# A two-layer hybrid encoder on one core: bias sums taken early, transposes of value blocks deferred, gate stores issued by GpSimd

## The chip, the core and the metric

The kernel runs on one core of a Trainium2 chip. A core has a matrix engine (TensorE; the profile has PE for its products and PEld for its weight loads), three engines for element-wise work (VectorE, in the profile DVE; ScalarE, ACT; GpSimd, POOL), SyncE (SP), which here only issues transfers, and 16 DMA engines. Each engine carries out its own instructions in their order, and waits on semaphores for the others. The metric is the time of one execution on the device in microseconds (us); of several runs the median is given.

## The reference

The program is two layers of a bidirectional encoder over 512 tokens of width 1024. Cut to what matters here:

```python
h = x
for l in range(DEPTH):                                   # 2 layers
    h = h + 0.5 * rmsnorm(swiglu(rmsnorm(h, ..), ..), ..)
    u = rmsnorm(h, mix_pre_g[l])
    qa, ka, va, qb, kb, vb, qc, kc, vc, gl = split(u @ w_in[l])   # one projection
    oa = neighbourhood_attention(qa, ka, va, na_rpb[l])  # 8 heads of 64, bias and mask added to scores
    ob = sliding_window_attention(rope(qb), rope(kb), vb, sw_sink[l])
    oc = differential_attention(rope(qc), rope(kc), vc, ...)
    yb = einsum(stack([oa, ob, oc]), w_branch[l])
    merged = sum(sigmoid(gl + b_gate[l]) * yb, axis=2)   # three gates of width 1024
    h = h + rmsnorm(merged @ w_out[l], mix_post_g[l])
    h = h + 0.5 * rmsnorm(swiglu(rmsnorm(h, ..), ..), ..)
```

In the neighbourhood attention the bias of a head is looked up by the distance of query and key on a grid of 8 by 64 tokens, and keys outside a window of 16 columns are masked with -1e30. `sigmoid(z)` is computed as (1 + tanh(z/2))/2, so a gate is one tanh on ScalarE.

## The kernel before

All values are float32. A product of two float32 matrices is made of three products: each operand is split into a high part and what is left of it, a low part, and high x high, low x high and high x low are added up in a PSUM bank (L326, L327 and L328 in one helper, L680 in another). ScalarE makes the high parts, VectorE the low ones.

A layer goes through four phases, each with a pool of memory of its own: the first feed-forward part, the projection (`project`), the mixer (`mixer`) and the second feed-forward part. In the profiled execution the projection of the first layer lies at about 370 to 510 us and its mixer at 508 to 860; those of the second layer at 1545 to 1690 and 1690 to 2040.

**The projection.** The 30 column blocks of 128 for queries, keys and values are made here. Eight of them (`COVER`) are plain products, the other 22 go in 11 groups of two blocks (`GROUPS`), by a scheme with seven products in place of eight (class `Seven`, products p1 to p7, L680). Its sums need many more steps on VectorE: sums of weights (L621, L640, L644) and low parts (L630, L654, L658, L667), and sums of products (L733, L738). PSUM has eight banks: two "mm", two "mx", three "at" and one "o". During the groups two of the "at" banks hold sums of the groups (`seed_banks`), so one is left for everything else.

A finished block is copied out of PSUM by ScalarE in halves or whole (`evict`, L1398) and handed to `ready`. Blocks of queries and keys are split and stored in DRAM for later (`stacked`, `store`, whose stores GpSimd issues at L1405). Value blocks (VA, VB, VC) go through `turned`: four transposes on PE into a bank "at" (L1432), and then a copy to a high part by ScalarE (L1438) and a subtraction on VectorE (L1439) for each of two halves, and stores. Blocks of the second branch that need a rotation put four steps into a list `slowly`; after each group `work(3)` runs three steps of that list, and what is left is run when the last group is done. `tables_of_a`, called in group 6's turn, loads a tile `pre` of tag "n" (two buffers, outside the phases' pools): the masks (L1549, L1550) and the bias tables of heads 0 and 1 (L1552).

**The mixer.** The table `ORDER` sets the order in which its units are written: `qa1` loads the operands of two heads of the neighbourhood attention (branch a), `aa1` is that attention, `kb`, `qb`, `ab` and `qc`, `ac`, `fc` belong to branches b and c, `ga3` is block 3 of gate a, `ya3` block 3 of the merge of branch a. A unit for two heads of branch a (`qkv_a`) asks for the bias tables of its heads (`ask`, tile `braw`, L1726; for heads 0 and 1 they are in `pre`), then loads its stacks: operands `st` whose upper half is the high part and whose lower half is the low part, four transfers of 128 KB a head, at L1776 and L1777 (`restacked`), and the value parts `x` (L1753). `biases` adds bias and mask with four steps on VectorE (L1737), into two tiles of the mixer's pool. `softmax_pv` then makes the scores (L1672), adds the bias and takes the maximum (L1675), takes the exponential (L1684 on ScalarE) and divides by the sum (L1692, or L1694 on VectorE); its second half, run after the next head's scores, transposes the probabilities (L1703), splits them (L352 and L353) and multiplies by the values (L1706, L1707). For the other branches a rotation loads a block and a copy with halves swapped (`sh`, L1761) and combines them (L1762 to L1764).

A gate block is a product of 24 matrix steps (L326 to L328) and one tanh (L1909). Gate a's blocks stay on chip, in two tiles of tag "n". The blocks of gates b and c are stored in DRAM, 256 KB each, by SP at L1912, 16 a layer, and loaded back when they are merged (`combine`; the sums of branch b on GpSimd at L1926).

**What sets the order.** The kernel is written as one sequence; a scheduler then decides the order of each engine's instructions, and adds the waits. A transfer issued by SP, ACT or GpSimd stands in that engine's order, and if it must wait, for its data, for its buffer, or for an earlier transfer that uses the same completion semaphore, everything behind it on that engine waits too. Weight loads (`wr`, L211) are issued by SP in the projection and by ACT in the mixer.

## Time and profile before

| | us |
|---|---|
| median of 3 runs (2383.48 to 2388.46) | 2384.1 |
| the profiled execution | 2380.2 |
| its span | 2378.4 |
| PE busy in the span | 2346.9 |
| DVE busy | 1883.2 |
| ACT busy | 1448.5 |
| POOL busy | 178.8 |

The span goes from the first to the last instruction of the profiled execution; some 1.8 us lie around it. Rows of a timeline read: start, duration, engine, line, operation, output and inputs, and in square brackets how long the engine was idle before and what released it. In a table of waits a row reads: who waited, for what, total us, times, longest. "SPq" and "ACTq" are transfers that the engine issues. The engine order below is of the built program and has no times in it.

### The profile page before, as it was taken

What the parts mean: (1) busy time and instruction counts of PE and PEld (TensorE: products, weight loads), DVE (VectorE), ACT (ScalarE), POOL (GpSimd) and SP (SyncE); (2) the same over time, 40 slices, a digit from 0 to 9 for tenths busy, and PEclk for the clock granted to TensorE, in tenths of its full rate; (3) what the DMA queues carried; (4) which work ended last, traced back from release to release, by engine and by line L of the source; (5) the groups of instructions that cost most, each with busy time, mean ns of one, the idle gap of its engine ahead of it and who ended that gap; (6) DMA issues with size and microseconds to landing.
All of it is one profiled execution on the core that took longest, in us unless ns stands there. A gap on an engine that the chain in (4) does not pass through costs nothing. (4 is left out here: it accounts for less than half of the span.)

```text
span 2378.4 us, 39981 instructions
## 1 busy us (share of the span) xinstructions
PE 2346.9 (99%) x15062; PEld 2105.4 (89%) x15062; DVE 1883.2 (79%) x3056; ACT 1448.5 (61%) x2711; POOL 178.8 (8%) x242
## 2 busy tenths in 40 slices
PE   9999999999999999999999999999999999999998
PEld 8999889987888789998899998899878878899987
DVE  7887987967977577888878878889589766788796
ACT  6565566668766365655655554666687664556563
POOL 0111001110000101110001110011000010011100
PEclk9999999999999999999999999999999999999999
DMA  5566446667565534664525565376766664346642
GB/s 170 161 169 192 153 142 197 207 205 214 164 186 177 158 100 141 170 159 166 174 87 169 160 178 195 107 218 207 210 188 175 171 201 131 106 144 170 192 144 87
DMA packets 143264, 395.13 MB, mean 166 GB/s; under 512 B 19296, under 2 KB 26080, under 8 KB 142560
## 3 DMA queue, kind: packets, MB, share of 16 engines
q1 hardware_dynamic: 114672, 279.25, 37.8%
q0 software_dynamic: 12992, 57.68, 9.4%
q10 hardware_dynamic: 15408, 55.66, 7.7%
q8 instruction: 118, 1.93, 0.3%
q14 instruction: 74, 0.61, 0.1%
HBM read 326.98 MB, written 80.74 MB: 171 GB/s over the span
## 5 line engine op out<-in xcount | busy, mean ns | idle before, releaser
L680 PE MATMUL mm<-X,h 128*128 128x256 f32 x1472 | 261.6, 277 | 0.2
L224 ACT ACTIVATE w<-wr 128x512 fp32r<-128x512 f32 x272 | 167.7, 627 | 119.9 <-PE mm L328 67.9
L225 DVE TENSOR_TENSOR w<-wr,w 128x512 fp32r<-128x512 f32 x272 | 190.9, 710 | 59.7 <-ACT w L224 58.8
L326 PE MATMUL mm<-X,w 128*128 128x512 f32 (+1 forms) x602 | 228.5, 380 | 2.0 <-ACT X L553 1.8
L327 PE MATMUL mm<-X,w 128*128 128x512 f32 (+1 forms) x602 | 227.8, 378 | 0.8 <-DVE X L554 0.7
L328 PE MATMUL mm<-X,w 128*128 128x512 f32 (+1 forms) x602 | 226.4, 377 | 0.0
L680 PEld LDWEIGHTS mm<-X,h 128*128 128x128 f32 x1472 | 223.6, 188 | 1.2 <-DVE v L738 0.5
L680 PE MATMUL mm<-ht,l 128*128 128x256 f32 x736 | 205.9, 280 | 0.0
L680 PE MATMUL mm<-ht,h 128*128 128x256 f32 x736 | 205.5, 279 | 0.0
L680 PE MATMUL mm<-lt,h 128*128 128x256 f32 x736 | 204.8, 278 | 0.0
L680 PE MATMUL mx<-ht,h 128*128 128x256 f32 x736 | 203.7, 277 | 0.0
L680 PE MATMUL mx<-lt,h 128*128 128x256 f32 x736 | 203.6, 277 | 0.0
L680 PE MATMUL mm<-X,l 128*128 128x256 f32 x736 | 203.6, 277 | 0.0
L680 PE MATMUL mx<-ht,l 128*128 128x256 f32 x736 | 203.4, 276 | 0.0
L630 DVE TENSOR_TENSOR l<-wr,h 128x1024 fp32r<-128x1024 f32 x92 | 112.5, 1223 | 62.7 <-PE mm L680 62.6
L662 ACT ACTIVATE h<-wr 128x1024 fp32r<-128x1024 f32 x92 | 97.7, 1062 | 73.6 <-PE mx L680 52.6
L680 PE MATMUL at<-X,w 128*128 128x256 f32 x1104 | 141.1, 277 | 0.0
L680 PEld LDWEIGHTS mm<-ht,l 128*128 128x128 f32 x736 | 138.7, 188 | 0.1
L680 PEld LDWEIGHTS mm<-lt,h 128*128 128x128 f32 x736 | 138.7, 188 | 0.0
L680 PEld LDWEIGHTS mm<-ht,h 128*128 128x128 f32 x736 | 138.6, 188 | 0.0
L680 PEld LDWEIGHTS mx<-lt,h 128*128 128x128 f32 x736 | 138.3, 188 | 0.0
L680 PEld LDWEIGHTS mx<-ht,h 128*128 128x128 f32 x736 | 138.1, 188 | 0.2
(449 smaller groups left out, 6748.2 us busy)
## 6 DMA issues: line engine op xcount, KB each, us to landing
wr<-in_wts_dram SPq DMA_DIRECT2D x269, 512.0 KB
wr<-in_wts_dram ACTq DMA_DIRECT2D x106, 512.0 KB
sum<-in_wts_dram POOLq DMA_DIRECT2D x64, 512.0 KB, 4.9
st<-part SPq DMA_DIRECT2D x120, 128.0 KB
ap<-in_wts_dram SPq DMA_DIRECT2D x20, 512.0 KB
a<-kept SPq DMA_DIRECT2D x32, 256.0 KB
ap<-sum SPq DMA_DIRECT2D x16, 512.0 KB
x<-part SPq DMA_DIRECT2D x32, 256.0 KB
```

The source lines that it names most:

```text
L224: A.activation(hi, raw, AF.Copy)
L225: V.tensor_tensor(out=lo, in0=raw, in1=f(hi), op=ALU.subtract)
L326: PE.matmul(acc, w[0], x[0], start=start, stop=False)
L327: PE.matmul(acc, w[0], x[1], start=False, stop=False)
L328: PE.matmul(acc, w[1], x[0], start=False, stop=stop)
L630: V.tensor_tensor(out=w["l1"], in0=self.raws[g][0], in1=f(w["h1"]), op=ALU.subtract)
L662: A.activation(self.W[g]["h24"], self.raws[g][1], AF.Copy)
L680: PE.matmul(acc, ws[i], xs[j], start=start and k == m == 0, stop=stop and k == n - 1 and m == 2, skip_group_check=True,)
```

## The change

The diff has five parts: (1) in `ORDER`, the first two gate blocks are gb0 and gb1, and ga0, ga1 and others follow later; (2) the bias sums of heads 0 and 1 go into a new tile `edges`, the second tile of tag "n", in place of tiles of the mixer's pool; (3) `qkv_a` asks for bias tables after the stacks and values; (4) the stores of gates b and c are issued by GpSimd; (5) `turned` for value blocks is put in the list `slowly`.

```diff
--- before.py
+++ after.py
@@ -70,8 +70,8 @@
 
 
 ORDER = """
-qa0 qa1 aa0 ga0 ga1 qa2 aa1 ga2 qa3 aa2 ga3 gb0 kb qb0 aa3 gb1 qb1 ab0
-gb2 gb3 qb2 ab1 gb4 gb5 gb6 qb3 ab2 gb7 ga4 qc0 ab3 ga5 ga6 qc1 ac0
+qa0 qa1 aa0 gb0 gb1 qa2 aa1 ga0 qa3 aa2 ga1 ga2 kb qb0 aa3 ga3 gb2 qb1
+ab0 gb3 qb2 ab1 gb4 gb5 gb6 qb3 ab2 gb7 ga4 qc0 ab3 ga5 ga6 qc1 ac0
 ga7 ya0 gc0 ya1 qc2 fc0 ac1 gc1 ya2 gc2 ya3 gc3 fc1 qc3 ac2 ya4 ya5
 ya6 ya7 yb0 gc4 fc2 ac3 yb1 gc5 yb2 gc6 fc3 yb3 gc7 yb4 yb5 yb6 yb7
 yc0 yc1 yc2 yc3 yc4 yc5 yc6 yc7
@@ -1467,9 +1467,9 @@
             elif QB <= c < VB:
                 turned_by(c, x)
             elif c < QB or c == VB:
-                turned(c, x, 2)
+                slowly.append(lambda: turned(c, x, 2))
             elif c >= VC:
-                turned(c, x, 1)
+                slowly.append(lambda: turned(c, x, 1))
             else:
                 made[c] = store("raw", x)
 
@@ -1551,6 +1551,7 @@
             for hd in range(2):
                 nc.sync.dma_start(t[:, 2 + hd, :], raw_of(l, hd))
             made["tables"] = t
+            made["edges"] = sb.tile([P, 4, T], F32, tag="n", name=nm("edges"), bufs=BUFS["n"])
 
         def gate_tile(c):
             if (c - GL) % 4 == 0:
@@ -1727,8 +1728,12 @@
 
         def biases(hd):
             raw = raws.pop(hd)
-            edge = big("g", name="bedge")
-            mid = big("g", shape=(P, 2 * P), name="bmid")
+            if hd < 2:
+                edge = made["edges"][:, hd, :]
+                mid = made["edges"][:, 2, 2 * P * hd : 2 * P * (hd + 1)]
+            else:
+                edge = big("g", name="bedge")
+                mid = big("g", shape=(P, 2 * P), name="bmid")
 
             def put(dst, mask, n0, n1):
 
@@ -1799,9 +1804,10 @@
 
 
         def qkv_a(p):
+            got = restacked(QA + p, False), restacked(KA + p, True), values(VA + p)
             for s in range(2):
                 ask(2 * p + s)
-            return restacked(QA + p, False), restacked(KA + p, True), values(VA + p)
+            return got
 
         oa = [sb.tile([P, 4, T], F32R, tag="X", name=nm("oa"), bufs=BUFS["X"]) for _ in range(2)]
 
@@ -1909,7 +1915,7 @@
                 A.activation(t, pg, AF.Tanh, scale=0.5, bias=col("b_gate", l, n * KD + m))
                 if n:
                     d = dr.tile([P, T], F32, tag="gate", name=nm("gate"), bufs=4 * KD)
-                    nc.sync.dma_start(d, t)
+                    G.dma_start(d, t)
                     t = d
                 gate[n, m] = t
```

How this moves instructions is seen at three places. Lines behind the edited ones have numbers higher by one to six after the change (L1737 becomes L1742, L1726 becomes L1727, L1753 L1758, L1761 L1766, L1776 and L1777 L1781 and L1782, L1912 L1918). The numbers in names are those of buffers and tell the same tile of another; names of the two programs can't be compared by number.

**PE, transposes of the last deferred groups of the first layer's projection.** Before, a block (x803) is transposed in two pairs, as its halves come:

```order
L680 MATMUL mm791_5230<-X539_3649,h24785_5213 128x256
L680 MATMUL mm791_5230<-X538_3648,l24793_5245 128x256
L1432 MATMUL at819_5417<-cons_66,x803_5331 128x128 x2
L680 MATMUL mm811_5363<-ht2608_4128,h24806_5351 128x256
L680 MATMUL mm811_5363<-lt2609_4129,h24806_5351 128x256
L1432 MATMUL at819_5417<-cons_66,x803_5331 128x128 x2
L680 MATMUL mm811_5363<-ht2608_4128,l24813_5378 128x256
```

After, the block (x804) and the block of values with it are transposed four at a time, one after the other, behind other products:

```order
L680 MATMUL mm826_5486<-ht1595_4069,h13817_5398 128x256
L680 MATMUL mm826_5486<-lt1596_4070,h13817_5398 128x256
L680 MATMUL mm826_5486<-ht1595_4069,l13821_5433 128x256
L1432 MATMUL at845_5615<-cons_66,x804_5332 128x128 x4
L1432 MATMUL at850_5628<-cons_66,v799_5269 128x128 x4
L680 MATMUL mm855_5641<-X536_3646,h1829_5503 128x256
```

The four transposes of a block stand together, and two blocks stand one right behind the other, in two banks (at845, at850), since a group's sum has left one by then.

**DVE, projection of the first layer, behind the first deferred value block** (at648 and at649 are the transposed blocks 0 and 1 of branch a's values that were put off; L621 to L667 split weights; L1742 are the moved bias sums). After the change:

```order
L667 TENSOR_TENSOR l24656_4384<-wr631_4234,h24647_4342 128x1024
L644 TENSOR_TENSOR wr646_4328<-r13658_4389,wr645_4326 128x512
L738 TENSOR_TENSOR v641_4277<-mm634_4240,v641_4277 128x256
L654 TENSOR_TENSOR w12666_4431<-wr646_4328,w12666_4431 128x512
L1439 TENSOR_TENSOR early566_3957<-at648_4344,early566_3957 128x4x64
L658 TENSOR_TENSOR wr646_4328<-wr646_4328 128x512
L1459 TENSOR_TENSOR x616_4176<-x616_4176,sh617_4178 128x512
L1439 TENSOR_TENSOR early566_3957<-at648_4344,early566_3957 128x4x64
L1742 TENSOR_TENSOR edges791_5230<-pre790_5225 128x256
L1742 TENSOR_TENSOR edges791_5230<-pre790_5225 128x128 x2
L1439 TENSOR_TENSOR v650_4358<-at649_4353,v650_4358 128x4x64
L630 TENSOR_TENSOR l1660_4405<-wr645_4326,h1657_4386 128x1024
```

On PE the transposes into at649 stand 25 products behind those into at648, and they wait for the second of the two L1439 that read at648. Between the bias sums five others stand earlier, ahead of the L621 that takes wr631. Before, all bias sums stood on DVE behind the end of the projection, each head's right ahead of its L1675.

**SP, start of the first layer's mixer.** Before, two bias tables (braw) are loaded ahead of each two heads' stacks:

```order
L211 DMA wr848_5616<-in_wts_dram 128x1024
L1726 DMA braw877_5796<-in_rpb_dram 128x1x512
L1726 DMA braw878_5798<-in_rpb_dram 128x1x512
L1776 DMA st879_5800<-part589_4051 64x512
L1777 DMA st879_5800<-part590_4053 64x512
L1776 DMA st880_5803<-part589_4051 64x512
...
L1753 DMA x885_5818<-part614_4158 128x512
L1753 DMA x886_5820<-part615_4160 128x512
L1726 DMA braw929_6000<-in_rpb_dram 128x1x512
L1726 DMA braw930_6002<-in_rpb_dram 128x1x512
L1776 DMA st931_6004<-part669_4444 64x512
```

After, behind them:

```order
L211 DMA wr839_5591<-in_wts_dram 128x1024
L1781 DMA st878_5797<-part588_4042 64x512
L1782 DMA st878_5797<-part589_4044 64x512
L1781 DMA st879_5800<-part588_4042 64x512
L1782 DMA st879_5800<-part589_4044 64x512
...
L1758 DMA x884_5815<-part652_4364 128x512
L1758 DMA x885_5817<-part653_4366 128x512
L1727 DMA braw886_5819<-in_rpb_dram 128x1x512
L1727 DMA braw887_5821<-in_rpb_dram 128x1x512
L1781 DMA st929_6002<-part664_4427 64x512
```

The first stack loads stand right behind the last weight load of the projection, and a pair of bias loads stands behind 14 loads of stacks and values.

**SP again, loads for the rotated blocks** (raw, x and sh are a rotated block, its load and its swapped copy). Before, with gate stores between them:

```order
L1912 DMA gate1172_6863<-gate1171_6861 128x512
L1777 DMA st1179_6902<-part810_5361 64x512
L1776 DMA st1180_6905<-part809_5359 64x512
L1777 DMA st1180_6905<-part810_5361 64x512
L1776 DMA st1246_7172<-part852_5636 64x512
L1777 DMA st1246_7172<-part853_5638 64x512
L1753 DMA x1306_7403<-raw778_5146 128x512
L1761 DMA sh1307_7405<-raw778_5146 32x512 x2
L1912 DMA gate1178_6900<-gate1177_6898 128x512
L1776 DMA st1247_7175<-part852_5636 64x512
L1777 DMA st1247_7175<-part853_5638 64x512
L1761 DMA sh1307_7405<-raw778_5146 32x512 x2
```

After, without gate stores, and with the copy's loads (sh1304) among stacks that stood earlier:

```order
L1758 DMA x1303_7400<-raw778_5146 128x512
L1766 DMA sh1304_7402<-raw778_5146 32x512 x2
L1781 DMA st995_6226<-part727_4755 64x512
L1782 DMA st995_6226<-part728_4757 64x512
L1781 DMA st996_6229<-part728_4757 64x512
L1782 DMA st996_6229<-part727_4755 64x512
L1758 DMA x997_6232<-part709_4680 128x512
L1766 DMA sh1304_7402<-raw778_5146 32x512
L1758 DMA x998_6234<-part710_4682 128x512
L1781 DMA st1058_6463<-part679_4513 64x512
```

All stores of gates (L1918) now stand in GpSimd's order, twelve a layer ahead of the first sum of L1926 and four among those sums.

## The prediction

> **What bounds the kernel now.** I read the busy times first, then what TensorE (PE) waits for over the whole run, then the timeline of each stall, then the chain of waits, which names what stands behind a stall.
>
> ```profile
> span 2378.4 us, 39981 instructions
> PE 2346.9 (99%) x15062; PEld 2105.4 (89%) x15062; DVE 1883.2 (79%) x3056; ACT 1448.5 (61%) x2711; POOL 178.8 (8%) x242
> ```
>
> PE is busy in all but 2378.4 - 2346.9 = 31.5 us. The change adds and removes no matrix product, so it can only win from these 31.5 us, or lengthen them. PE's waits, summed over the run (total, times, longest):
>
> ```profile
> PE mm L326 <- DVE x L1922: 4.9, 3, 2.3
> PE at L1432 <- ACT x L1398: 3.3, 3, 1.4
> PE o L1707 <- DVE lo L353: 3.1, 5, 1.5
> PE at L1703 <- ACT s L1692: 2.8, 2, 1.5
> PE mx L1672 <- DMA st<-part: 0.7, 1, 0.7
> ```
>
> The first row is the end of the mixer, which the change leaves alone. The other four lie where the change works: L1432 are the transposes of the value blocks in the projection, L1703, L1707 and L1672 the attention. They add up to 3.3 + 3.1 + 2.8 + 0.7 = 9.9 us: the most that can be won.
>
> **1. Transposes of value blocks among the deferred steps.** The timeline of PE at one of the three waits of L1432:
>
> ```profile
> 477.97 0.38 PE L1432 MATMUL at<-cons,x 128*128 128x128 f32 x2
> 478.11 0.37 PE L680 MATMUL mm<-ht,h 128*128 128x256 f32 x1
> 480.00 0.44 PE L1432 MATMUL at<-cons,x 128*128 128x128 f32 x2 [1.40 <-ACT x L1398]
> ```
>
> Two of the four transposes of a block go, then PE stands 1.40 us for the second half of the block, which ACT is still copying out (L1398). In the order of the change the four stand together, behind the next group's products, where the block has long been copied: -3.3 us.
>
> What is late next: a bank. Of the three banks "at" the group sums hold two, so the transposes share one until the last groups, and the change puts two blocks (at648, at649) 25 products apart, with at649 waiting until DVE has read the second half of at648 (L1439). The rows that price it:
>
> ```profile
> 408.79 0.28 PE L680 MATMUL mm<-ht,h 128*128 128x256 f32 x1
> 410.15 0.28 PE L680 MATMUL mx<-ht,h 128*128 128x256 f32 x1
> 398.94 0.42 DVE L1439 TENSOR_TENSOR v<-at,v 128x256 fp32r<-128x256 f32 x1
> 402.52 0.68 DVE L654 TENSOR_TENSOR w<-wr,w 128x512 fp32r<-128x512 f32 x1
> 405.99 0.42 DVE L738 TENSOR_TENSOR v<-mm,v 128x256 f32<-128x256 f32 x1
> ```
>
> Twelve products take 410.15 - 408.79 = 1.36 us, so PE wants the bank 0.4 + 25 x 0.113 = 3.2 us after the product that L738 reads. DVE, which goes in order, has in that time L738, L654, L1439, L658, L1459 and the second L1439: 0.42 + 0.68 + 0.42 + three more by the same rows (two of 0.68, one of 0.42) = 3.3 us, with the overlap of 0.08 each 2.9. DVE makes it only if it comes to L738 no later than 0.3 us after PE. If it is late by x, PE stands x - 0.3. Lower end 0; upper end the whole 2.9 us of queue; I take 1.2, since the bias sums below stand ahead of it on DVE, and 0.3 for a second such pair (at701): 1.5 us in each of two layers, +3.0. So this part nets -3.3 + 3.0 = -0.3 us (-3.3 to +2.9).
>
> **2. Bias sums of heads 0 and 1 moved into the projection.** The prices, where they stood, at the start of the mixer, are:
>
> ```profile
> 514.90 0.43 DVE L1737 TENSOR_TENSOR bedge<-pre 128x256 f32<-128x256 f32 x1 [2.35 <-DMA part<-lo]
> 515.98 0.42 DVE L1675 CUSTOM_DVE_ANT_0 s<-mx,bedge 128x256 f32<-128x256 f32 x1
> 400.00:420.00 20.00, 20.00 (x175) 19.82 (x174) 18.89 (x26) 13.50 (x28) 3.42 (x7) 1.00 0.60 198
> 404.85 1.23 DVE L621 TENSOR_TENSOR r<-wr,wr 128x1024 f32<-128x1024 f32 x1 [0.92 <-DMA wr<-in_wts_dram]
> 406.32 1.22 DVE L667 TENSOR_TENSOR l<-wr,h 128x1024 fp32r<-128x1024 f32 x1
> ```
>
> A head's four sums take 515.98 - 514.90 = 1.08 us, two heads 2.16. DVE waited 2.35 us there, for the projection's memory, but PE stood nowhere near it (its first stall in the mixer comes 20 us later), so taking that wait away wins 0. Where they go, DVE was busy 18.89 of 20 us (columns: PE, PEld, DVE, ACT, POOL, clock, share of the DMA engines, GB/s). Five of the eight sums (1.42 us) stand before L621, which had 0.92 us of idle time before it; so DVE is 0.5 us late there, and 0.74 more with the last three. The weights that L667 ends at 407.5 PE takes up at 408.79, 1.25 us later, which covers it: 0 by itself, and the lateness of 0.5 to 1.24 is what the 1.2 above stands for. The cover goes if the loads of pre come late: DVE would stand with all weight splitting behind it.
>
> ```profile
> 381.52 1.68 SPq L1552 DMA_DIRECT2D pre<-in_rpb_dram  x2
> 386.49 0.34 SPq L211 DMA_DIRECT2D wr<-in_wts_dram  x1
> ```
>
> The change puts one of the two loads of L1552 behind the weight load of 386.49, so it starts near 387; DVE wants it near 403 (L654 of 402.52 stands ahead). 16 us of margin: 0.
>
> **3. Bias loads behind the stacks, gate stores by GpSimd.** The two stalls of L1703 (1.5 and 1.3 us) come from ACT, which issues a weight load and waits in its place. ACT, then the chain of waits in the second layer, then SP's queue:
>
> ```profile
> 535.93 0.33 ACTq L211 DMA_DIRECT2D wr<-in_wts_dram  x1
> 536.31 1.71 ACT L1692 ACTIVATE s<-s,l 128x256 f32<-128x256 f32 x4 [3.09 <-DMA wr<-in_wts_dram]
> 1702.48 9.45 DMA wr<-in_wts_dram
> 1712.35 1.71 ACT s L1692 x4
> SPq L1726 <- DMA part<-hi: 27.4, 1, 27.4
> 514.31 0.66 SPq L1726 DMA_DIRECT2D braw<-in_rpb_dram  x1
> 520.00:540.00 20.00, 18.54 (x109) 15.70 (x108) 12.74 (x44) 15.30 (x47) 0.00 (x0) 1.00 0.87 224
> 540.00:560.00 20.00, 19.89 (x111) 16.31 (x110) 17.71 (x58) 18.67 (x53) 0.00 (x0) 1.00 0.91 248
> ```
>
> A weight load issued at 1702.48 took 9.45 us; the next may not go until it has landed, and ACT with it, and the softmax (L1692) behind it. It is slow because SP stood 27.4 us before a bias load (braw) and then let go everything behind it at once: the DMA engines are 0.87 and 0.91 busy there. In the new order the first stack loads stand ahead of that bias load, and the weight loads meet other transfers at their turn. If all of that spreads, -2.8; if the crowd only shifts, 0. The same bytes are to be moved, from the same point on, so I take -2.0. The bias load itself comes after 14 loads of 0.59 us each, 8 us later:
>
> ```profile
> 519.45 0.59 SPq L1777 DMA_DIRECT2D st<-part  x1
> 528.16 0.42 DVE L1737 TENSOR_TENSOR bedge<-braw,pre 128x256 f32<-128x256 f32 x1
> ```
>
> The first stack load goes at 514.3 then, the bias load near 522.5, and DVE wants it at 528.2: covered if it lands within 5.7 us, and with the 9.45 us of the crowded load it would be late by 3.8, of which PE's gate products hide what they can. I price it at 0, and keep +2 a layer for the upper end.
>
> The stall of L1707 is DVE's wait for a rotated copy (sh) that SP was late to load:
>
> ```profile
> 577.69 0.89 SPq L1761 DMA_DIRECT2D sh<-raw  x2
> 581.10 0.34 SPq L1912 DMA_DIRECT2D gate<-gate  x1
> 582.77 2.28 SPq L1761 DMA_DIRECT2D sh<-raw  x2
> 589.18 0.69 DVE L1763 TENSOR_TENSOR sh<-sh,sinR 128x512 f32<-128x512 f32 x1 [2.69 <-DMA sh<-raw]
> 591.60 0.39 PE L1707 MATMUL o<-lo,x 128*128 128x256 f32 x1 [1.53 <-DVE lo L353]
> SPq L1912 <- ACT gate L1909: 39.4, 9, 10.6
> PE o L1707 <- DVE lo L353: 1.0, 2, 0.7
> ```
>
> Between the halves of sh stands a gate store that waits for ACT's tanh (such stores held SP 39.4 us between 500 and 800). With the stores on GpSimd nothing of the kind is between them, and they stand far ahead: -1.5, and -0.7 for its like in the second layer (the last row: L1707's waits from 1700 to 1790). L1672's wait for a stack, behind SP too: -0.7. Together -2.9; with nothing won, 0.
>
> GpSimd pays by this row:
>
> ```profile
> L1405 POOL DMA_DIRECT2D part<-hi x30 | 16.3, 544 | 425.6 <-ACT hi L1410 423.0 <-ACT h L662 2.3
> ```
>
> 32 stores of 0.54 us are 17 us on an engine that is 8% busy, and idle through 520 to 560: 0. Should the sums of the merge (L1926, on GpSimd) stand behind a store that waits, it is one store to a sum, 0.5 us each.
>
> [...]
>
> **4. The order of gates.** gb0 and gb1 go first, ga0 and ga1 later, and head 2's scores come behind more gate products. No product is added; but the pairing of softmax and gates is drawn anew, and each stall of before was one such pairing (0.7 to 1.5 us). I put +1.0 for new ones (0 to +3).
>
> **Sum.** -0.3 + 0 - 2.0 - 2.9 + 1.0 = -4.2 us on the profiled execution, whose time is 2380.2 (span 2378.4 and 1.8 around it): 2376.0. The median of the runs shown is 2384.1, 3.9 above that execution; with the same 3.9 the change comes to 2379.9, say **2380 us**. What a measurement of this kernel can tell from no change is about 0.2%, 4.8 us, so the forecast lies just inside "same".
>
> **Rivals.**
> *All waits go.* The bank comes free in time and the crowd disperses: -3.3 - 2.8 - 2.9 = -9.0, with 0 to +1 new: 2375 to 2376. For it: DVE came to L738 just as PE ended in before. Against it: 18.89 of 20 us.
> *The crowd only shifts, and the bank takes what the transposes give.* -0.3, -2.9, and a late bias load or new pairings of 3: near 2384. For it: 0.91 of the DMA engines. Against it: what starts the crowd, SP's 27.4 us at one load, is a matter of order, and the order changes there. [...]
> *DVE becomes the bound in the projection.* Place: rows L1742 to L1439, 400 to 420 us. Price: bias sums of 2.16 us against 1.11 us of room, then the bank behind them, up to 2.9 us a layer, 5.8 for both, with the three later pairs of deferred blocks adding 0.3 each a layer, 7.6 in all, less the 3.3 won: +4.3; nothing won in the mixer and +3 of new pairings there: +7.3, 2391. It decides from the point where DVE reaches L738 more than 2.5 us behind PE. For it: DVE's 18.89; against it: 1.25 us of weights in hand, and idle time (0.92) just where the sums go.
> *The change doesn't do what it says.* The transposes' wait for ACT comes back at another place, since the last group's blocks are still run together at the end of the projection: the 3.3 us stay, and so does what the bank costs where blocks are deferred (3.0), against 4.9 won in the mixer and 1.0 of new pairings: 2384.1 + 3.0 - 4.9 + 1.0 = 2383.
>
> **How the numbers follow.** Forecast (-1.5 to -7, own range 2377 to 2383) 0.42, a third of it beyond -4.8; all waits go 0.2; the crowd shifts 0.2; DVE the bound 0.13; not as said 0.05. Faster: 0.2 + 0.14 and a little of the rest = 0.36; slower: 0.13 + a part of the third case = 0.18; same 0.46. Range: 2375, less 1 for what is uncertain in its terms, takes in the first rival; upward it goes to 2389, most of the way to the 2391 of the slower one, with the two others inside: 2374 to 2389.
>
> **What would show it.** Right: no row L1432 <- ACT x in PE's waits, no L1703 <- ACT s at the mixer's start, no ACT wait for wr of 3 us, no SP wait at a gate store, sh loaded before DVE wants it. The bank: a new row L1432 <- DVE L1439 near 407 and its like near 1585; its size decides between forecast, first rival and third. Wrong would be: L680 waiting for DVE L630 to L667 in the projection, softmax rows waiting for braw, or a mixer whose stalls stand elsewhere with the same sum.

## The result, and the profile after

The changed kernel takes 2406.4 us (median of 5 runs, 2396.4 to 2410.6) against 2384.1 for the kernel before: a ratio of 1.0089, with a 95% interval of 1.0072 to 1.0106. It is 22 us slower, where 4 us less were forecast. Its profiled execution took 2403.0 us. The head of its page:

```profile
span 2401.2 us, 39994 instructions
PE 2351.5 (98%) x15062; PEld 2106.8 (88%) x15062; DVE 1882.4 (78%) x3056; ACT 1439.9 (60%) x2707; POOL 197.9 (8%) x274
```

The span is 22.8 us longer: PE idles 2401.2 - 2351.5 = 49.7 us in place of 31.5, and is "busy" 4.6 us longer on the same 15062 products. What it waited for, summed over the run:

```profile
PE o L1708 <- DVE lo L353: 9.6, 4, 3.7
PE at L363 <- DVE msc L1948: 7.6, 4, 2.3
PE at L1432 <- DVE early L1439: 3.7, 2, 2.2
PE mx L1863 <- ACT e L1870: 3.5, 2, 2.0
PE mm L680 <- ACT at L719: 3.2, 3, 2.4
...
```

The waits that the forecast meant to remove are gone: no row of L1432 for ACT's L1398 (3.3 us before), none of L1704 for ACT's softmax (2.8). In their place stand others. Summing such rows over stretches of both layers gives this picture, which all later runs are read against. "Projection" goes from its start to the first scores, "mixer A" is the 75 us from there, "mixer B" the 270 us after; the numbers are us of PE waits in the one execution that was profiled, and the whole run includes what lies outside these stretches.

| kernel | projection | mixer A | mixer B | whole run |
|---|---|---|---|---|
| before | 3.3 | 4.7 | 9.3 | 26.3 |
| the change | 8.6 | 7.9 | 18.7 | 44.5 |

In the **projection** the bank is what was feared, and more. VectorE and ScalarE around the first deferred pair, and PE behind them:

```profile
404.92 0.36 ACT L1438 ACTIVATE early<-at 128x256 fp32r<-128x256 f32 x1
405.18 1.05 ACT L635 ACTIVATE h<-r 128x1024 fp32r<-128x1024 f32 x1
408.03 0.38 ACT L1438 ACTIVATE early<-at 128x256 fp32r<-128x256 f32 x1 [1.81 <-DVE early L1439]
408.31 0.38 ACT L719 ACTIVATE at<-mm 128x256 f32<-128x256 f32 x1
...
407.58 0.42 DVE L1439 TENSOR_TENSOR early<-at,early 128x256 fp32r<-128x256 f32 x1
409.12 0.41 DVE L1439 TENSOR_TENSOR early<-at,early 128x256 fp32r<-128x256 f32 x1
...
409.68 0.52 PE L1432 MATMUL at<-cons,x 128*128 128x128 f32 x3 [2.17 <-DVE early L1439]
```

The two engines take turns: ScalarE copies a half, VectorE subtracts it, ScalarE copies the second half only then, VectorE subtracts it, and only then is the bank free. ScalarE stands 1.81 us in this chain.

The longest stall of the second projection, 2.39 us ending at 1588.21, is another matter: it lies 12 us ahead of that layer's bank wait. PE waits there for L719, ScalarE's copy of a group's first product sum:

```profile
1585.56 1.23 DVE L621 TENSOR_TENSOR r<-wr,wr 128x1024 f32<-128x1024 f32 x1 [1.24 <-DMA wr<-in_wts_dram]
1586.82 1.06 ACT L635 ACTIVATE h<-r 128x1024 fp32r<-128x1024 f32 x1 [3.22 <-DVE r L621]
1587.79 0.37 ACT L719 ACTIVATE at<-mm 128x256 f32<-128x256 f32 x1
```

VectorE could not sum the weights (L621) until they had been loaded, ScalarE stood for that sum (L635), and L719 stands behind L635 in ScalarE's order. The runs with part 5 alone, below, show where this comes from.

In **mixer A** VectorE waits for a bias table, 4.32 us, and PE behind it:

```profile
555.68 1.32 SPq L1727 DMA_DIRECT2D braw<-in_rpb_dram  x2
563.26 0.42 DVE L1742 TENSOR_TENSOR bedge<-braw,pre 128x256 f32<-128x256 f32 x1 [4.32 <-DMA braw<-in_rpb_dram]
564.14 0.58 PE L1708 MATMUL o<-lo,x 128*128 128x256 f32 x1 [3.72 <-DVE lo L353]
```

And in **mixer B** it waits for blocks to be rotated. VectorE's waits over the run, of before and then of the change:

```profile
DVE sh L1763 <- DMA sh<-raw: 8.2, 8, 2.7
DVE x L1762 <- DMA x<-raw: 3.7, 2, 2.1
```

```profile
DVE x L1767 <- DMA x<-raw: 19.9, 8, 3.4
DVE bedge L1742 <- DMA braw<-in_rpb_dram: 8.4, 3, 4.3
DVE edges L1742 <- DMA pre<-in_rpb_dram: 3.7, 2, 2.1
```

The waits for the swapped copy (sh) have gone, as forecast; those for the block itself (x<-raw) have grown from 3.7 to 19.9 us.

What is left are the 4.6 us in which PE is busy longer. The granted clock (the eighth column, after PE, PEld, DVE, ACT and POOL) shows them, in stretches of 2 us around the stall that ends at 409.68:

```profile
408.00:410.00 2.00, 0.32 (x3) 0.35 (x4) 2.00 (x6) 0.66 (x2) 0.00 (x0) 1.00 0.50 201
410.00:412.00 2.00, 2.00 (x12) 2.00 (x11) 0.69 (x3) 1.04 (x3) 0.52 (x1) 0.55 0.03 8
412.00:414.00 2.00, 2.00 (x13) 2.00 (x12) 1.53 (x3) 1.29 (x3) 0.02 (x1) 0.60 0.33 135
414.00:416.00 2.00, 2.00 (x20) 2.00 (x19) 2.00 (x4) 1.43 (x5) 1.38 (x3) 1.00 0.65 119
```

After the stall of 2.17 us the clock is at 0.55 and 0.60 for 4 us, and PE makes 12 and 13 products where it makes 20 at full clock: 2 x (0.45 + 0.40) = 1.7 us lost beside the stall. In stretches of 20 us the clock is 0.91 at two places before the last stall of the run in the kernel before, and at five in the change (400, 560, 660, 1580 and 1880): three more, 5.1 us, which is about the 4.6. Summed over all stretches of 20 us, what the clock takes, 20 x (1 - clock), is 7.8 us in before and 12.2 in the change.

### The profile page after: what moved, and what is told of

Its sections match the earlier page's. It is cut to its first block, busy times and chain, and to the rows that moved or that the text cites. A ratio compares the mean times of both kernels' runs of the same rounds, so it can differ in the third digit from the quotient of the medians.

```text
span 2401.2 us, 39994 instructions
## 1 busy us (share of the span) xinstructions
PE 2351.5 (98%) x15062; PEld 2106.8 (88%) x15062; DVE 1882.4 (78%) x3056; ACT 1439.9 (60%) x2707; POOL 197.9 (8%) x274
## 3 DMA queue, kind: packets, MB, share of 16 engines
q0 software_dynamic: 15552, 66.07, 10.2%
## 5 line engine op out<-in xcount | busy, mean ns | idle before, releaser
L621 DVE TENSOR_TENSOR r<-wr,wr 128x1024 f32<-128x1024 f32 x92 | 112.6, 1224 | 33.5 <-DMA wr<-in_wts_dram 27.3
```

The lines of the kernel that those rows point to most:

```text
L621: V.tensor_tensor(out=w["r13"], in0=base, in1=r[0], op=ALU.add)
```

## The experiments

The parts are numbered as in the diff: 1 and 2 the order of units and the early bias sums (they belong together, since the gates' tiles follow the sums' tile), 3 the bias tables behind the stacks, 4 the gate stores by GpSimd, 5 the deferred transposes. Ratios are to the kernel before, run beside each, with 95% intervals.

### One part undone

The theory was that the loss is made at the three places above, each by its own part; the rivals put it elsewhere or at one of them.

```diff
-                slowly.append(lambda: turned(c, x, 2))   # e_no5: part 5 undone
+                turned(c, x, 2)
-                    G.dma_start(d, t)                     # e_no4: part 4 undone
+                    nc.sync.dma_start(d, t)
-            got = restacked(...), ...; ask(...)           # e_no3: part 3 undone
+            ask(...); return restacked(...), ...
-                edge = made["edges"][:, hd, :]            # e_no12: parts 1 and 2 undone
+            edge = big("g", name="bedge")
```

> The change with its fifth part undone (value blocks are transposed at once again). Theory: half of the loss is made in the projection, by the shared bank and by VectorE late behind the moved bias sums; without deferral the bank waits (2.2, 1.5 and 0.6 us) go and the old waits of L1432 for ScalarE (3.3 us) come back, so the projection's stalls fall from 10.9 to about 6 us: 5 us faster than the change, near 2401 as a median. Rival A (the mixer alone loses): the same time as the change. Rival B (the bias sums on VectorE alone make the projection's stalls): still 6 us of ScalarE L719 and VectorE L738 waits there, 2 us faster at most.

> The change with its fourth part undone (gate stores issued by SyncE again). Theory (loads that SyncE issues in another order reach VectorE late): gate stores on SyncE do no good, so the same time as the change or 0 to 4 us slower. Rival (stores from GpSimd crowd the DMA engines or build their transfers slowly, and so make the loads late): 8 us or more faster than the change, with the waits of VectorE for braw and x shorter.

> The change with its third part undone (bias tables asked for ahead of the stacks). Theory: VectorE's waits for braw (4.3 us at 563 and 4.0 us in the second layer) go, and with them PE's stalls of 3.9 and 0.6 us at 564 and 570 and of 1.7, 2.0 and 0.6 us at 1752 to 1758: 8 us faster than the change. Rival (the pairing of gates and scores makes these stalls): they stand elsewhere, the same time.

> The change with its first and second parts undone together (old order of units, bias sums of heads 0 and 1 in the mixer). Theory: the waits of VectorE for x<-raw (3.0 and 7.1 us in the first layer, 9.8 in the second) come from the new order of units, and PE's stalls behind them (2.6, 2.4, 0.9, 1.7, 1.1 and 1.8 us from 660 to 800, 11.3 us in the second layer) go for the old ones of 3.2 and 6.3 us; the projection loses its ScalarE L719 waits too (3 us): 15 us faster than the change, near 2391. Rival (deferral and late bias tables carry the loss): no more than 4 us faster.

| undone | median us | ratio | projection | mixer A | mixer B | whole run |
|---|---|---|---|---|---|---|
| (nothing: the change) | 2406.4 | 1.0089 (1.0072 to 1.0106) | 8.6 | 7.9 | 18.7 | 44.5 |
| 5 | 2388.9 | 1.0027 (1.0014 to 1.0040) | 5.2 | 2.3 | 18.1 | 35.4 |
| 4 | 2395.8 | 1.0044 (1.0028 to 1.0061) | 11.4 | 13.7 | 3.5 | 37.7 |
| 3 | 2404.3 | 1.0087 (1.0071 to 1.0103) | 10.0 | 9.6 | 10.2 | 38.5 |
| 1 and 2 | 2403.7 | 1.0082 (1.0065 to 1.0099) | 10.1 | 10.9 | 8.1 | 37.9 |

Undoing the deferral wins 0.62%, some 15 us, far more than the 5 expected: beside the projection it relieves mixer A, where VectorE's waits for bias tables fall from 8.4 to 2.1 us. Undoing the gate stores wins 11 us where nothing, or a loss of up to 4, was expected; that is the size of the rival there, and its cause, that the stores slow the loads, is tested below (e_4x). Mixer B falls from 18.7 to 3.5 us, but mixer A rises. My theory named the wrong part for mixer B. Undoing part 3, or 1 and 2, was expected to win 8 and 15 us and wins nothing: the waits named go or shrink, others come. Why they win no time although the waits fall by 6 us is in the clock. The page of the kernel with part 3 undone, and two of its stretches of 20 us:

```profile
PE 2357.6 (98%) x15062; PEld 2114.9 (88%) x15062; DVE 1884.4 (78%) x3056; ACT 1445.6 (60%) x2711; POOL 198.7 (8%) x274
```

```profile
400.00:420.00 20.00, 17.27 (x124) 16.90 (x123) 15.88 (x26) 10.50 (x23) 3.23 (x6) 0.83 0.47 149
560.00:580.00 20.00, 16.49 (x79) 13.28 (x78) 13.87 (x45) 16.47 (x48) 0.00 (x0) 0.83 0.86 263
```

PE's busy time is 6 us above that of the change: at 0.83 a stretch loses 3.4 us, twice what one at 0.91 does, and there is a third at 0.83 (1760). Over all stretches up to 2400 the clock takes 15.8 us here and 10.6 in the change. With 1 and 2 undone PE is busy 4.9 us longer than in the change.

### One part alone

> Before with the fifth part alone (value blocks' transposes deferred). Theory: the 3.3 us of L1432 for ScalarE go, and bank waits of 1 to 2 us a layer take their place, smaller than in the change since no bias sums stand ahead on VectorE: -2 to +2 us against before. Rival A (deferral is free without the bias sums): -3.5 us. Rival B (the bank alone costs what the change showed): +1 to +4 us.

> Before with the fourth part alone (gate stores issued by GpSimd). Theory: SyncE no longer stands before a gate store, the load of sh comes in time and the stalls of L1707 (1.5 and 0.7 us) go: -2 us, -4 to 0. Rival (GpSimd's stores make loads late): +5 us or more.

> Before with the third part alone (bias tables behind the stacks). Theory: VectorE waits in place for braw, as in the change: +3 to +8 us, with a wait of VectorE for braw of 2 us or more in each layer. Rival (the new order of units has moved heads' scores to where the loads are late, and with the old order they arrive in time): within 2 us of before, the softmax stalls of L1703 gone.

> Before with the first and second parts together (new order of units, bias sums of heads 0 and 1 early in a tile of their own). Theory: most of the mixer's loss is here: +8 to +15 us, with VectorE's waits for x<-raw of 10 us or more over both layers, and 3 us in the projection from VectorE's sums. Rival (loads are late only because the bias tables were put behind the stacks): within 3 us of before.

| alone | median us | ratio | projection | mixer A | mixer B | whole run |
|---|---|---|---|---|---|---|
| (nothing: before) | 2384.1 | 1 | 3.3 | 4.7 | 9.3 | 26.3 |
| 5 | 2394.2 | 1.0035 (1.0020 to 1.0050) | 11.8 | 3.3 | 12.3 | 38.0 |
| 4 | 2389.1 | 1.0025 (1.0013 to 1.0036) | 3.5 | 6.2 | 16.9 | 35.1 |
| 3 | 2392.5 | 1.0032 (1.0021 to 1.0043) | 3.1 | 9.4 | 8.9 | 31.0 |
| 1 and 2 | 2383.2 | 0.9988 (0.9976 to 1.0000) | 3.6 | 10.4 | 8.3 | 32.4 |

Now each part shows its place. Parts 3, 4 and 5 each cost a quarter to a third of a percent by themselves, part 4 against a forecast of -4 to 0 us; 1 and 2, in which I had put most of the mixer's loss, cost nothing. (Their row of waits is of the slowest of ten executions, 2387.6 us.) The four sum to 0.80%, near the 0.89% of the whole, but that is no proof that they add up: undoing part 3 won nothing, undoing part 5 won 0.62%, and parts 1 to 3 together, below, are faster than before.

With 1 and 2 alone VectorE's waits for x<-raw rise as expected, from 3.7 to 12.1 us, and mixer B's PE waits do not (8.3 us). So a late rotation is not by itself a loss; it depends on what stands behind it on VectorE.

Part 5 costs 0.35% without any bias sums on VectorE, more than any of the three sizes expected for it (4 us at most); so the sums are not what makes the projection stall (rival B of e_no5). PE's waits with part 5 alone:

```profile
PE mm L680 <- ACT at L719: 4.6, 3, 2.4
...
PE at L1432 <- DVE early L1439: 4.0, 2, 2.7
...
PE mm L680 <- DVE v L738: 2.8, 3, 2.0
```

The bank's 4.0 us are less than the 7.4 us of the group's own sums (L719, L738) that ScalarE and VectorE are late with. Those do not stand behind the bank. The longest, 2.35 us, ends at 400.12, 12 us ahead of the bank's wait in that layer (411.96). VectorE and ScalarE there with part 5 alone, and then ScalarE in before:

```profile
396.96 1.22 DVE L621 TENSOR_TENSOR r<-wr,wr 128x1024 f32<-128x1024 f32 x1 [4.32 <-DMA wr<-in_wts_dram]
398.21 1.06 ACT L635 ACTIVATE h<-r 128x1024 fp32r<-128x1024 f32 x1 [3.05 <-DVE r L621]
399.70 0.37 ACT L719 ACTIVATE at<-mm 128x256 f32<-128x256 f32 x1
```

```profile
397.87 0.37 ACT L719 ACTIVATE at<-mm 128x256 f32<-128x256 f32 x1
399.05 1.06 ACT L635 ACTIVATE h<-r 128x1024 fp32r<-128x1024 f32 x1 [0.52 <-DVE r L621]
```

The sum of weights (L621) is made no later than in before, where it starts at 397.80. But in before L719 stands ahead of L635, and with part 5 it stands behind it, and so waits for the weights too. The longest wait for L738 (2.03 us, ending at 424.56) is of the same kind: on VectorE it stands behind an L621 that waited 3.06 us for weights, and no L621 of before's projections waited longer than 1.2 us. So taking the transposes out of their place has also changed the order and the waits of the steps around them.

Part 4 alone makes mixer B wait. VectorE at one rotated block, with gate stores by GpSimd, and then at the same block in before:

```profile
689.79 0.69 DVE L1762 TENSOR_TENSOR x<-x,cosR 128x512 f32<-128x512 f32 x1 [2.79 <-DMA sh<-raw]
690.40 0.68 DVE L1922 SCALAR_TENSOR_TENSOR gate<-gate,mm 128x512 f32<-128x512 f32 x1
691.00 0.17 DVE L1942 RECIPROCAL msc<-msc 128x4 f32<-128x4 f32 x1
```

```profile
680.85 0.18 DVE L1942 RECIPROCAL msc<-msc 128x4 f32<-128x4 f32 x1 [0.51 <-ACT msc L1941]
683.06 0.75 DVE L1944 SCALAR_TENSOR_TENSOR oc<-oc,misc,at 128x512 f32<-128x512 f32 x1 [2.03 <-PE at L363]
683.72 0.69 DVE L1762 TENSOR_TENSOR x<-x,cosR 128x512 f32<-128x512 f32 x1
```

In before the reciprocal that PE's spread (L363) waits for stands ahead of the rotation (L1762); with part 4 it stands behind it, and the rotation waits 2.79 us for its load. The edit of this run touches neither: it moves only the sixteen stores a layer from SyncE's queue, and with them gone the scheduler has laid VectorE's order anew.

### Taking one cause away

Four edits test the causes: deferred transposes by turns in the banks "at" and "o" (e_5o); deferral for the groups' blocks only (e_5late); the loads of the second rotated block written ahead of the stacks of the first (e_4x); and parts 1 to 3 without 4 and 5 (e_123).

```diff
-            tp = bank("at")                                   # e_5o
+            tp = bank(("at", "o")[len(turns) % 2])
-                slowly.append(lambda: turned(c, x, 2))        # e_5late
+                turned(c, x, 2) if c in COVER else slowly.append(lambda: turned(c, x, 2))
-            return stacks(rope(QC + hd), False), stacks(rope(KC + hd), True), ...   # e_4x
+            q = split(rope(*loads(QC + hd)), "tx")
+            k = loads(KC + hd)
+            q = stacks(q, False)
+            return q, stacks(split(rope(*k), "tx"), True), ...
```

> Before with the fifth part, but the deferred transposes go by turns into a bank at and into the bank o, which is idle in the projection. Deferral alone made before 0.35% slower and its projections' stalls 10 us longer in the profile. Theory (one shared bank: PE waits for VectorE's second L1439, and VectorE and ScalarE are late to the sums of groups behind it): the waits of L1432 for L1439 (4.0 us) go, and most of L719 (4.6) and L738 (2.8) with them, so 6 us or more faster than deferral alone, 0 to -4 us against before. Rival A (VectorE and ScalarE are simply late: the deferred steps and the groups' steps fall together there): the L1432 waits go but L719 and L738 stay or grow; 4 us faster than deferral alone at most. Rival B (the scheduler's other order makes it): no gain.

> Before with only the groups' own value blocks deferred; those of the first eight blocks (VA, VA+1, VB) are transposed at once as before. Theory: the two bank waits lie at the first deferred pair (2.7 and 1.4 us in the profile of deferral alone), so they go, and half of the loss: 4 us faster than deferral alone, or more. If the old waits of L1432 (3.3 us) also stay away, 0 to -3 us against before. Rival A (all pairs cost alike): 0.25% slower than before still.

> The same as e_5late, whose profiled execution was a disturbed one of 7504 us, for a profile: no wait of L1432 for L1439 and at most 1 us of L719 or L738 in the first projection, the old waits of L1432 for L1398 gone or below 1 us.

> Before with the fourth part (gate stores by GpSimd), and the loads of the second rotated block written ahead of the stacks of the first. With gate stores alone VectorE stood 19.6 us for x<-raw, against 3.7. Theory (with the stores off SyncE the scheduler puts that load behind the stacks of the block before): VectorE's waits for x<-raw fall to below 8 us, and the loss of 0.25% goes: -3 to +2 us against before. Rival (GpSimd's stores slow the loads themselves): the waits stay above 12 us, and the loss stays.

> The change without its fourth and fifth parts: order of units, early bias sums, bias tables behind the stacks. Theory (effects add by place: deferral costs in the projection, gate stores in the middle of the mixer, and bias tables behind the stacks take away the waits for stacks that early sums laid bare): its first 75 us of the mixers stall 3 us in all in place of 14 with parts 1 and 2 alone; 2 to 8 us faster than before. Rival (part 3 costs 0.3% wherever it stands, as it did alone): 2 to 8 us slower than before.

**A second bank** (e_5o): 2389.9 us, 1.0023 (1.0011 to 1.0035). The waits of the second transposes for L1439 fall from 4.7 us to 1.0, but PE still waits 4.1 us for L719 and 2.0 for L738, and that in a profiled execution (2383.6 us) faster than the median. The ratio falls from 1.0035 to 1.0023, a third of the loss, with intervals that overlap. So the bank is a part of the matter, and not the larger one. That L719 and L738 stay is what rival A expected, but not for its reason: before the first of these stalls VectorE is not busy with deferred steps, it stands idle for weights (3.29 us, until 395.64), and L719 stands behind L635 here too.

**Deferring later blocks only** (e_5late): 2383.5 us, 0.9998 (0.9988 to 1.0007). The cost is gone. A profile of it (2380.7 us, one run) has in place of 11.8 us of projection waits 1.9:

```profile
PE mm L680 <- ACT at L719: 1.0, 1, 1.0
...
PE at L1432 <- ACT x L1398: 0.4, 1, 0.4
```

On ScalarE L719 (398.42) stands ahead of L635 (399.28) again. The old waits of L1432 for ScalarE are gone too (3.3 to 0.4), as the forecast wanted, yet the median is not below before's.

**Rotated loads ahead** (e_4x): 2383.4 us, 1.0000 (0.9991 to 1.0010). VectorE's waits:

```profile
DVE x L1765 <- DMA x<-raw: 3.7, 5, 2.6
DVE sh L1766 <- DMA sh<-raw: 1.1, 1, 1.1
```

The loss of part 4 goes with the late loads, from 14.3 (x<-raw) and 5.3 us (sh<-raw) to these, while the stores are still GpSimd's; so the rival, that these stores slow the loads, is out. This edit, too, lets the scheduler lay a new order, so it shows that the late rotation is the loss, not that the place in SyncE's queue alone makes it late.

**Parts 1 to 3** (e_123): 2379.6 us, 0.9985 (0.9975 to 0.9995). A little faster than before, and no different from 1 and 2 alone (0.9988): part 3, which costs 0.32% alone, costs nothing once heads 0 and 1 have their sums early. With 1 and 2 alone PE stands 7.0 us for stacks, and SyncE 27.7 us at one bias table ahead of them; part 3 takes PE's 7.0 us away. But mixer A comes to 9.1 us, where 3 were expected, all of it behind one new wait of VectorE in each layer. In the first:

```profile
567.59 0.53 SPq L1918 DMA_DIRECT2D gate<-gate  x1
568.17 0.43 SPq L1766 DMA_DIRECT2D sh<-raw  x1
574.73 0.69 DVE L1768 TENSOR_TENSOR sh<-sh,sinR 128x512 f32<-128x512 f32 x1 [5.18 <-DMA st<-part]
576.60 0.39 PE L1708 MATMUL o<-lo,x 128*128 128x256 f32 x1 [4.55 <-DVE lo L353]
```

It is the wait of the forecast's third part: the last load of one sh stands in SyncE's queue behind a gate store and stacks, 16 us after the others (551.59). The row puts the wait down to a stack load issued among them; its like in the second layer (5.20 us) is put down to the gate store. Parts 1 to 3 make it worse (5.18 us for 2.69), and with part 4 it is not there.

### The menders in the change

> The whole change, with the loads of the second rotated block written ahead of the stacks of the first. Theory (rotated loads behind stacks carry the mixer's loss): VectorE's waits for x<-raw (19.9 us in the change) fall below 8 us and the late part of both mixers (16.5 us of larger PE stalls) to about 9: 8 to 12 us faster than the change, near 2396. Rival (the loads stay late for another cause once all parts are there): less than 3 us.

> The whole change, with the transposes of VA, VA+1 and VB run at once and only those of the groups deferred. Theory (the first deferred pair in one bank carries the projection's loss): the projections' larger PE stalls fall from 10.9 to 6 us or less, and the wait for braw at the start of the mixer is shorter since SyncE gets there earlier; 10 to 15 us faster than the change, near 2393, or as without deferral (2389). Rival (any deferral costs this): less than 4 us.

> The change without its fifth part, and with the loads of the second rotated block ahead. Theory (effects add): without deferral the change stood at +0.27%, and the rotated loads were all that was left of the loss: 0.2 to 0.4% faster than before, near 2376, with no wait of VectorE for x<-raw over 2 us. Rival: within 0.1% of before or slower, since other loads are late then.

> All five parts with both menders: only the groups' value blocks deferred, and the loads of the second rotated block ahead. Theory: as the kernel without deferral, less up to 3 us for L1432's old waits: 0.2 to 0.5% faster than before, near 2374. Rival (deferral costs something even so): slower than the same without the fifth part by 3 us or more.

> The fastest version (parts one to four with the rotated loads ahead, -0.43%) with its gate stores by SyncE again. Theory (gate stores on SyncE make VectorE wait 5.2 us for sh in each layer, as with parts 1 to 3 alone): 3 to 6 us slower than with GpSimd's stores, near -0.2%. Rival (once the rotated loads stand ahead, who issues the gate stores makes no difference): within 2 us of it.

| kernel | median us | ratio | projection | mixer A | mixer B | whole run |
|---|---|---|---|---|---|---|
| c_x: the change, rotated loads ahead | 2391.8 | 1.0046 (1.0028 to 1.0064) | 9.3 | 5.9 | 10.6 | 35.4 |
| c_l: the change, later blocks only deferred | 2389.7 | 1.0029 (1.0018 to 1.0041) | 1.4 | 1.8 | 22.1 | 33.7 |
| e_mended: both | 2379.7 | 0.9995 (0.9969 to 1.0021) | 2.2 | 6.7 | 9.9 | 27.1 |
| e_1234x: rotated loads ahead, part 5 left out | 2373.3 | 0.9957 (0.9942 to 0.9972) | 3.3 | 2.4 | 10.7 | 25.9 |
| e_123x: the same, gate stores by SyncE | 2381.3 | 0.9997 (0.9983 to 1.0012) | 5.5 | 7.6 | 7.1 | 29.4 |

Each mender takes more from the whole change (0.43% and 0.60%) than its part cost alone, and in the place where it should: c_x brings mixer B from 18.7 to 10.6, c_l the projection from 8.6 to 1.4. Both together bring it level with before, so the first eight blocks' deferral and the late rotation are the loss against before. They are not all that the parts cost: e_mended was expected to beat the same kernel without part 5 (e_1234x, the next paragraph), and its median is 6.4 us higher, as the rival had it (the two intervals just touch). On top of before, deferring the groups' blocks cost nothing (e_5late); here it does, with 6.7 us of waits in mixer A against 2.4, and 8.1 us of VectorE's waits for bias tables against 2.3. Why is open.

The best is the change without the deferral and with the rotated loads ahead: 2373.3 us, 0.43% faster than before. The page of its profiled execution:

```profile
PE 2342.5 (99%) x15062; PEld 2103.8 (89%) x15062; DVE 1881.6 (79%) x3056; ACT 1448.1 (61%) x2711; POOL 197.7 (8%) x274
```

PE's waits are no fewer than before (25.9 against 26.3 us), VectorE still waits 3.8 us for x<-raw where none of 2 us was expected (the longest is 2.5), and PE's busy time is 4.4 us less. The clock does not explain that: over all stretches it takes 7.4 us here and 7.8 in before. So the win is measured, and its cause is not shown. One part of it is: with gate stores by SyncE (e_123x), the only difference, the time is 8 us longer, the waits of VectorE for sh of 5.2 and 3.7 us are back, and mixer A has 7.6 us of PE waits in place of 2.4. So part 4 does win what it was priced at and more, beside parts 1 to 3 and where the rotation isn't late; on top of before alone (e_4x) it won nothing.

## Why the prediction was wrong

**Bounds.** That only PE's idle time could be won or lost was wrong by the clock: in the change, five of the six stalls of 2.0 us or more (the last of the run left out) are followed by about 4 us at 0.50 to 0.70 of the clock. Each that is costs 1.7 us more than its row in the waits, in "busy" time.

**1. Deferred transposes: forecast -0.3 (-3.3 to +2.9), the first step that failed.** The old waits did go (-3.3), the new one came at the place named, 2.2 us near 410 and 1.5 in the second layer, with 0.6 more: 4.3 for the 3.0 of the sum. The price of the pair by VectorE's queue alone left out that the chain goes through ScalarE twice. More was lost by a term that the sum did not have at all, the group's own steps: PE's waits for L719, L738 and L724 are 4.2 us in the change, 7.6 with the part alone, and none of L719 or L738 in the projections of before. The sum priced the transposes at their new place, and not what the new order does to the steps of other blocks: L719 now stands behind L635, which waits for weights. With two clock drops (0.91 at 400 and at 1580) the projections lost about 5.3 + 3.4 = 8.7 us in the change; with the part alone, which has drops at the same two places, 8.5 + 3.4 = 11.9 in the profiled execution, of a cost of 0.35% (8.4 us) over all runs. That the bias sums would make the lateness was wrong as well: alone, without them, the waits for L1439 are 4.7 us. (The upper end, +2.9, is one layer's queue; by its own terms it would have been 2 x 2.9 + 0.6 - 3.3 = +3.1.)

**2. Bias sums early: forecast 0.** They cost nothing by themselves (e_12), but the margin of 16 us for the loads of pre was not there, in either layer:

```profile
393.53 0.42 DVE L1742 TENSOR_TENSOR edges<-pre 128x256 f32<-128x256 f32 x1 [1.58 <-DMA pre<-in_rpb_dram]
1573.99 0.65 SPq L1552 DMA_DIRECT2D pre<-in_rpb_dram  x1
1583.89 0.42 DVE L1742 TENSOR_TENSOR edges<-pre 128x256 f32<-128x256 f32 x1 [2.08 <-DMA pre<-in_rpb_dram]
```

I had read the five early sums as standing near 403 us, next to the bank; they ran at 390.2 to 393.9, and the load that they wanted was issued at 385.04. VectorE stood 1.58 us, and 2.08 us in the second layer, where the load was taken up 9.9 us after it was issued. The forecast named this danger. It came, and it cost little: the L621 behind the sums had to wait for its weights in any case, 0.92 and 1.24 us more.

**3. Bias tables and gate stores: forecast -2.0 and -2.9, both steps half right.** ACT's wait before a weight load went and the stalls of 1.5 and 1.3 us with it; the wait for sh went. But the bias load that I let go at 0, "+2 a layer" at most, cost VectorE 8.4 us, not at the first pair of heads, whose margin I worked out, but at the last (555.68), where 7.6 us lie between issue and use. And gate stores were priced on GpSimd's and SyncE's queues, not by what else moves when they leave: 16 us more of waits for x<-raw.

In the runs the loss isn't in the transfers, since it goes with an order of loads while the stores stay on GpSimd (e_4x: VectorE's waits for x<-raw are 3.7 us, for 14.3 with part 4 alone). SyncE's 39.4 us for tanh are a wait in place, and they are what the 8 us between e_123x and e_1234x come from, as far as the waits for sh show (5.2 and 3.7 us).

**4. New pairings: forecast +1 (0 to +3); the gate stores and this term together are the most mis-sized.** Mixer B's waits rose from 9.3 to 18.7 us. I held that a change in the order of gates draws stalls anew by chance and at the old size. The order of gates (1 and 2 alone) leaves mixer B at 8.3 us; the gate stores (4 alone), forecast to win, bring it to 16.9, since with them off SyncE VectorE's steps are put where their loads are late, in the change eight times over.

**The rivals.** None came out. The nearest, VectorE as the bound in the projection, had the place and a price of +7, without ScalarE, without the clock, and without the mixer. The range ended at 2389; even all upper ends of the terms together (2.9 + 4 + 3 = 9.9) come to 2394. The late rotations, the new order of ScalarE's and VectorE's steps in the projection and the clock were in no term.

Open: the rotated loads ahead were not run on the kernel before alone, so how much of e_1234x's 0.43% is theirs isn't known; e_4x and e_123x, level with before, say that by themselves they do no more than pay for the rest. Why the groups' deferral costs some 6 us in e_mended and nothing in e_5late isn't known either. Nor was it settled why the scheduler, with the stores off SyncE, puts the rotation ahead of the reciprocal, or, with the transposes deferred, L635 ahead of L719; that it does is in the rows above.

## What to carry to other kernels

A step put off "to where there is room" must be priced on every engine it passes through and on its buffer, in the order in which the engines hand it on. Where a scheduler lays out the queues, taking work off one queue re-lays the others, so read the new order of the engines that wait in place (here VectorE's rotation against its reciprocal, and ScalarE's L635 against L719) before calling a move free. And when five edits come together, run each alone, and undo each: three of these lost a quarter to a third of a percent each by themselves, and one of those three won eight microseconds beside two others once the load that it made late was moved.

## What the runs showed that I had not expected

PE's granted clock was in no term of the forecast. In the changed kernel it fell after waits of 2.17, 2.39, 2.48 and 3.72 us, and after one of 2.00 (at 1888); it did not after one of 2.27 (at 702), nor after the bank's wait in the second layer, which ended at 1600.27 after 1.49 us:

```profile
1600.00:1602.00 2.00, 1.73 (x15) 1.76 (x16) 1.28 (x5) 0.57 (x2) 0.00 (x0) 1.00 0.00 0
```

So in this run the length of a stall does not decide it alone. With part 5 alone only two of seven stalls of 2.0 us or more (the last of the run left out), those of 2.35 and 2.70, were followed by a stretch below full clock.

The five falls in the changed kernel are alike: in stretches of 2 us the clock is 0.50 to 0.55 in the first behind the stall (from 410, 564, 666, 1588 and 1888), 0.60 to 0.70 in the second and 1.00 in the third.

The five runs of the changed kernel scatter over 14 us, with mean clocks of 0.992 in 2409.8 us and 0.996 in 2396.4, and the five of before beside them over 5. That would fit falls of the clock that come in some executions and not in others; only one execution was profiled, so it is not shown. The 17 runs of before beside e_1234x scatter over 14 us too, with mean clocks of 0.996 in 2391.9 us and 0.999 in 2378.0.
